# New step orders for the loops of an attention kernel on one core

## The chip, the cores and the metric

One of the eight cores of a Trainium2 chip runs the kernel. The metric is the device time of one execution in microseconds (us). A median of several executions is given, and one further execution was recorded by the hardware profiler; that one has its own span, from the first to the last instruction.

## The reference

Thirty-two sequences of different lengths (64 to 511 rows out of 512, 512 columns each) go through a projection to queries, keys and values, and through attention with eight heads of 64. Rows past a sequence's length are zero in the output.

```python
for b in range(batch):                        # 32
    x_b = x[b, :lengths[b]]
    q, k, v = split(x_b @ w_qkv, 3)           # each 8 heads of 64
    scores = q @ k.T / sqrt(64)               # for each head
    attn = exp(scores - max) / sum(exp(scores - max))
    output[b, :lengths[b]] = concat(attn @ v) # the rest of output[b] is 0
```

## The kernel before

**Tiling and stages.** The lengths are sorted on the chip, and the batches are worked on as sixteen pairs, longest first. There is one loop for each width: 512, 448, 384, 352 and so on down to 96 (LOOPS, L236). A loop runs as many times as there are pairs that need its width; for this draw 512, 448, 384, 320, 288, 256, 192, 128 and 96 run once, 224 and 160 twice, and 352 three times. A loop's body has two positions, one for each batch of its pair. A position (L1028) does the attention of its own batch and, between those steps, the projections of the batch that comes next. All inputs of TensorE are 16-bit (f16); its sums lie in eight PSUM banks of 512 columns, numbered 0 to 7.

**The steps.** The order of the steps in a position is written out by hand in a list of words (ORDER, L238 to L278), two positions separated by a bar. Every word is a step of TensorE with the copies or divides that follow it, or a step of another engine. The digits after @ are the banks that it writes.

- `S13@45`: group 13 of the scores, into banks 4 and 5 (L1269, L1259). The matmuls have 64 rows, since a head has 64; two heads run side by side in the two halves of the array's rows. ScalarE then takes the exponential of the banks (L1287).
- `Q2@1`, `K2@2`, `V1@6`: one projection each (q, k or values) as **single** matmuls over all 128 rows, four to a bank of 512 columns (qk at L1429, project at L300; val at L1484, values at L311). One copy takes the result to SBUF (L1442, L1489), on VectorE, or with a star (`K0*@7`) on ScalarE.
- `B1a@27 ... B1b:dd`: the same q and k blocks as **pairs** of 64-row matmuls (half_qk at L1360, halves at L1305, matmuls at L1323), one result in each of two banks. The pair comes in two halves, a and b (or three parts, a to c): a starts the sums and b adds the other rows to the same banks. `U0a ... U0b` are two value tiles as such a pair (half_values, L1379), `V0a ... V0b` a tile in halves, `W` the last value tile that two batches share (L1210 if single). The letters after the colon are the copy engines of the two results: d for VectorE, a for ScalarE.
- `A4@5`: value products (exponentials times values, 65 columns a matmul, the 65th giving the sum) as single 128-row matmuls (av at L1504, L1517). `A1a@67 ... A1b` are two heads, or groups of heads, as 64-row pairs (paired at L1599, L1631). `Z` adds the half-filled last tile (rest at L1544, L1557). VectorE then divides by the sums in three operations, R, U and O: reciprocal (L1706), live rows (L1712) and the product (L1715); if the two banks of a pair follow each other, the three operations serve both banks at once (both_normed at L1663, L1671 to L1693).
- `L` live rows, `P` mask and cast to f16 on GpSimd (L371), `D` load of a later x by DMA, `X` DMA transposes of the cast x (L328), `E0` a few columns that a narrower next loop leaves over (columns_left, L1453; its TensorE work only runs when a loop goes on).

**What sets the order of the engines.** The engines run their own instruction streams and wait for each other by semaphores. A planner (plan_waits, L41) goes through the head, the bodies of the loops and their entries in order (follow, L64), keeps for each bank and buffer who wrote it and who reads it, and plans a wait wherever an operation isn't already known to follow (L134 to L152). To hold in every loop alike, operations are named by rank, counted from the end of their position (by_rank, near L1865): O0 is the last divide of a position, G0 the last copy. A wait is given as a name and a number of positions back:

```python
wait = ("pos", o["name"], b - o["b"])
```

so a wait that a loop's own repetition needs is also carried out in its first iteration, where it stands for the operation of the same rank in the loop before. used_by (L1536) names the exponential buffers that a value product reads.

Of the kernel before, what the change touches and what calls it, by code (L numbers as in the profile page):

```python
# [18 lines left out]
P = 128  # L19
# [21 lines left out]
def plan_waits(head, bodies, entries, rare):  # L41
# [22 lines left out]
    def follow(chain):  # L64
        clock = defaultdict(lambda: defaultdict(int))
        seen = defaultdict(list)
        write, readers = {}, defaultdict(list)
        ahead = chain[0] == "head"
        came = -1 if ahead else chain[0]
        for at, v in enumerate(chain):  # L70
            if v == "head":
                todo = [("head", 0, k, op) for k, op in enumerate(head)]
                first = -1
            else:
                first = 2 * (chain.index(v) - ahead)
                todo = [(v, j, k, op) for j in range(2) for k, op in enumerate(bodies[v][j])]
                if at:
                    since = 0 if chain[at - 1] == "head" else chain[at - 1] + 1
                    lead = [(w, None, k, op) for w in range(since, v + 1) for k, op in enumerate(entries[w])]
                    todo = lead + todo  # L80
            for w, j, k, op in todo:
                b = -1 if v == "head" else 2 * (at - ahead) + (j or 0)
                mine = clock[op.eng]
                if op.skip and op.eng == "PE":
                    mine = defaultdict(int, mine)
# [64 lines left out]
                    learn(o)  # L150
                by = op.name if op.dma else op.eng
                count = (seen[by][-1]["count"] if seen[by] else 0) + 1  # L152
                after = dict(mine)
                after[by] = count
                o = {"name": op.name, "by": by, "count": count, "clock": after, "b": b}
                o |= {"dma": op.dma, "entry": j is None, "skip": bool(op.skip) and op.eng != "POOL" and not op.passed, "order": len(seen["all"])}
# [5 lines left out]
                    readers[r].append(o)  # L162
                for r in op.writes:
                    write[r] = o
                    readers[r] = []

    follow(["head"])
    for v in range(len(bodies)):
# [8 lines left out]
def kernel(  # L177
# [9 lines left out]
    B, MAXS, D = x.shape  # L187
# [15 lines left out]
    def ring(n, shape, dtype, name, pool=const):  # L203
# [32 lines left out]
    LOOPS = [512, 448, *range(384, 64, -32)]  # L236

    ORDER = {  # L238
        512: "L P D S0@12 U0a@65 S1@34 U0b:dd S2@01 B1a@27 S3@34 B1b:dd S4@56 S5@01 A0@3 A1@2 S6@45 B0a@76 "
        "S7@01 B0b:dd S8@23 U1a@54 S9@01 U1b:ad S10@23 B3a@76 S11@45 A2@0 S12@12 B3b:da S13@45 B2a@03 "  # L240
        "S14@12 S15@67 B2b:da A3@5 A4@2 A5@4 A6@0 X A7@7 | L P D S0@12 U0a@36 S1@45 U0b:ad S2@01 B3a@72 "
        "S3@34 B3b:dd S4@01 U1a@56 S5@34 A0@7 S6@01 U1b:dd S7@23 B0a@74 S8@01 B0b:dd S9@56 S10@23 A1@0 "
        "B2a@71 E0@4 S11@56 B2b:dd S12@23 A2@4 S13@56 A3@7 A4@3 S14@12 B1a@04 S15@67 B1b:ad A5@5 A6@3 X "
        "A7@0",
        448: "L P D S12@67 S13@45 B1a@32 S1@67 B1b:da S5@45 B0a@10 S3@67 B2a@23 S4@45 B0b:da B2b:dd S0@45 V1@6 "
        "S2@01 S6@23 S9@45 V2@7 A0@6 A2@0 Z0 S10@12 B3a@73 S7@45 B3b:da S8@12 A1@0 A3@6 S11@45 Z1 V0*@7 "
        "A4@1 A6@5 Z4 A5@4 X A7@7 Z5 | L P S0@23 S12@01 V1*@6 B2a@52 S1@34 B2b:dd S4@67 S3@01 W0@3 D "
        "S13@45 B1a@67 S6@12 B1b:dd S5@45 B0a@30 S2@12 B0b:dd S7@67 S8@45 V0@2 A0@7 A2@0 Z0 S9@45 S11@12 "
        "B3a@36 A3@7 A4@5 A1@4 Z1 S10@12 B3b:aa A5@0 E0@4 A7@1 A6@2 Z4 Z5 V2*@7 X",
        384: "L P D S0@34 B0a@65 B1a@72 S1@34 B0b:ad B1b:ad S2@01 B2a@43 S3@67 B2b:ad S4@01 A0@5 S5@23 B3a@76 "  # L250
        "S6@01 B3b:da S7@34 U0a@52 S8@01 S9@67 U0b:dd S10@34 A2@0 S11@67 A4@5 V2*@1 X A6@6 | L P D S0@23 "
        "B1a@47 S1@01 B1b:ad S2@23 B3a@56 S3@01 B2a@74 S4@23 B3b:dd S5@01 B2b:da A0@3 S6@12 S7@56 A2@4 "
        "U0a@70 S8@12 E0@3 S9@56 U0b:dd S10@12 B0a@43 S11@56 B0b:aa A4@1 A6@0 V2*@2 X",
        352: "L P D S0@56 V2*@4 S1@01 U0a@27 S2@56 S3@34 U0b:dd S4@01 B1a@65 S5@34 B1b:aa S6@01 A0@2 A2@7 "
        "S7@34 B2a@56 S8@01 B2b:aa S9@34 B3a@27 B0a@10 S10@56 B3b:dd S11@34 B0b:ad A4@6 X A6@5 | L P D "
        "S0@01 B0a@42 S1@67 B0b:da S2@01 B2a@53 S3@67 B3a@42 S4@01 B3b:da S5@67 B2b:da S6@01 A0@4 S7@67 "
        "U0a@25 S8@01 S9@34 U0b:ad B1a@10 S10@67 S11@34 B1b:ad A2@5 A4@7 A6@3 V2*@0 X",
        320: "L P D S2@12 S3@67 U0a@45 S4@01 S1@23 U0b:ad B0a@67 S8@12 B1a@30 S0@45 B0b:da B1b:dd S5@12 B3a@45 "
        "S7@67 B3b:da S9@23 A0a@10 S10@56 B2a@47 S6@23 A0b S11@56 B2b:aa A4@3 X A6@6 Z4 | L P S0@45 S7@12 "
        "W0*@7 D S1@34 B2a@50 S4@12 E0@7 B2b:dd S5@34 B3a@67 S2@12 B3b:aa B0a@43 S3@12 B1a@05 S8@67 "  # L260
        "B0b:da S6@12 B1b:ad A0a@76 S11@34 U0a@25 S10@01 A0b S9@34 U0b:aa A4@0 X A6@3 Z4",
        288: "L P D S0@56 B2a@24 S5@01 B2b:aa S3@67 B0a@01 S1@23 S9@45 B0b:dd S2@67 B1a@32 S6@45 B1b:da S4@67 "
        "B3a@10 S11@45 S8@23 B3b:ad U0a@76 A0a@05 S10@34 S7@12 A0b U0b:aa A6@3 X A4@4 Z4 | L P S5@01 "
        "U0a@27 S0@56 S1@01 U0b:dd S2@56 B3a@43 S6@01 B3b:aa W0a@52 D S10@01 E0@7 W0b:da B1a@34 S3@01 "
        "S4@67 B2a@25 B1b:da S8@01 B2b:da A0a@76 S7@34 S9@12 A0b B0a@05 S11@34 B0b:aa A4@1 X A6@7 Z4",
        256: "L P S0@34 U0a@02 S1@56 U0b:aa B0a@17 S2@34 S3@56 B0b A0a@02 B0c:da B1a@34 A0b B1b A1a@67 B1c:ad "
        "X D A1b | L P S0@01 U0a@25 S1@34 U0b:ad B0a@76 S2@01 E0@4 B0b A0a@23 B0c:da B1a@45 S3@01 A0b B1b "
        "A4@6 A6@7 B1c:aa X D",
        224: "L P B0a@30 S0@12 B0b B1a@45 B0c:da S1@67 B1b S2@01 U0a@23 S3@67 B1c:da U0b:da X D A0a@01 A1a@67 "
        "A0b A1b | L P B0a@45 S0@23 B0b B1a@01 S1@23 B0c:ad B1b S2@67 A0a@23 B1c:da U0a@54 S3@67 A0b "  # L270
        "U0b:aa X D A4@6 A6@7",
        192: "L P S0@01 S1@23 V0*@5 B0a@40 S3@67 B0b A0a@53 S2@12 A0b B1a@67 B0c:aa B1b A1a@21 B1c:ad X D A1b "
        "| L P B0a@50 S1@34 B0b S2@67 B0c:da W0@4 S0@12 B1a@03 S3@67 E0@5 B1b A0a@12 B1c:aa A0b A1a@46 "
        "V0a@57 A1b V0b:aa X D",
        160: "L P S0@01 S1@23 V0@5 Q0*@4 A0@0 K0*@7 A2@1 S2@23 Z0 K2*@6 Q2*@7 X D A4@5 A6@2 Z4 | L P S0@34 "
        "S1@67 K2@0 Q2*@1 A0@3 W0*@4 Q0@6 A2@5 K0*@0 Z0 S2@12 V0*@6 X D A4@4 A6@7 Z4",
        128: "L P S0@12 Q0*@6 K0*@0 V0@7 X D A0@6 A4@5 | L P S0@23 E0@7 Q0*@4 K0*@1 A0@34 V0*@2 X D",
        96: "L P S0@56 K0*@7 Q0*@4 V0@0 X D A0@56 | L P S0@12 Q0*@2 K0*@1 V0*@2 X D A0@34",  # L278
    }

    NARROW = (512, 448, 384, 320, 288, 256, 192, 128)
# [746 lines left out]
    def position(N, j, at, ring):  # L1028
# [11 lines left out]
        across = max(1, BANK // wide)  # L1040
# [188 lines left out]
        todo = [(i, kt) for i in range(NH // 2) for kt in range(n - quarters)]  # L1229
        lone = [(i, n - 1) for i in range(0, NH // 2, 2)] if quarters else []  # L1230
        todo = todo + lone
# [304 lines left out]
        def used_by(blocks, late=False):  # L1536
            if packed:
                mine = [todo.index(block) for block in blocks]
                mine = {min(k, len(todo) - 1) // across for b in mine for k in (b, b + 1)}
                return [f"et{j}.{k}" for k in sorted(mine)]  # L1540
            es = sorted({where[b + (0,)][0] for b in blocks})
            return [f"et{e}" for e in es] + [f"et{j}b"] * late
# [359 lines left out]
    def op_of(v, j, k):  # L1902
        return head[k] if v == "head" else (entries[v] if j is None else bodies[v][j])[k]
# [57 lines left out]
    for (v, j, k), todo in waits.items():  # L1961
        op = op_of(v, j, k)
# [81 lines left out]
    with tc.tile_critical():  # L2044
# [38 lines left out]
        for v, N in enumerate(LOOPS):  # L2083
# [17 lines left out]
            body, after = f"loop_{N}", f"after_{N}"  # L2101
            nc.br_lt(pair, ends[v], on_true=body, on_false=after)
            with nc.body(body):
# [6 lines left out]
                for j in range(2):  # L2110
                    for e in EN:
                        mine = [(k, op) for k, op in enumerate(bodies[v][j]) if op.eng == e]
# [54 lines left out]
```

## Time and profile before

| | us |
|---|---|
| median of 3 runs (lowest, highest) | 327.81 (327.38, 327.87) |
| span of the profiled execution | 328.5 |
| TensorE busy | 311.6 (95%) |
| ScalarE busy | 262.6 (80%) |
| VectorE busy | 197.7 (60%) |
| GpSimd busy | 101.9 (31%) |

The profile names the engines PE (TensorE matmuls), PEld (TensorE weight loads), DVE (VectorE), ACT (ScalarE), POOL (GpSimd) and SP (SyncE, which issues the DMAs). A line of the timeline gives the start, the duration, the engine, the line of the kernel, the operation, what it writes and reads, the size and the count; a bracket is the idle time ahead of it and what ended it. TensorE's matmuls are pipelined and their ends are modelled, so its durations overlap with the starts of the next ones. The span was 0.7 us longer than the median of the runs.

### The profile page before, as it was taken

What the parts mean: (1) busy time and instruction counts of PE and PEld (TensorE: products, weight loads), DVE (VectorE), ACT (ScalarE), POOL (GpSimd) and SP (SyncE); (2) the same over time, 40 slices, a digit from 0 to 9 for tenths busy, and PEclk for the clock granted to TensorE, in tenths of its full rate; (3) what the DMA queues carried; (4) which work ended last, traced back from release to release, by engine and by line L of the source; (5) the groups of instructions that cost most, each with busy time, mean ns of one, the idle gap of its engine ahead of it and who ended that gap; (6) DMA issues with size and microseconds to landing.
All of it is one profiled execution on the core that took longest, in us unless ns stands there. A gap on an engine that the chain in (4) does not pass through costs nothing.

```text
span 328.5 us, 13310 instructions
## 1 busy us (share of the span) xinstructions
PE 311.6 (95%) x5092; PEld 202.3 (62%) x5092; DVE 197.7 (60%) x635; ACT 262.6 (80%) x413; POOL 101.9 (31%) x148
## 2 busy tenths in 40 slices
PE   6899999999999999999999999999998999999980
PEld 4444645555655556556656657667777886777860
DVE  6777567566666646456455465545575565776853
ACT  4379999897878988988978989899867779687761
POOL 6448040324030330330231243043222224435320
PEclk9999999999999999999999999999999999999997
DMA  6984749395858999696676766857459857966651
GB/s 217 382 278 80 251 140 327 76 354 153 304 52 298 224 269 258 197 268 224 233 214 224 255 194 205 211 174 242 156 131 227 183 176 164 223 206 177 193 180 66
DMA packets 69449, 68.85 MB, mean 210 GB/s; under 512 B 40720, under 2 KB 40720, under 8 KB 69392
## 3 DMA queue, kind: packets, MB, share of 16 engines
q1 hardware_dynamic: 69344, 68.12, 71.4%
q8 instruction: 33, 0.54, 0.7%
q14 instruction: 24, 0.20, 0.2%
q10 hardware_dynamic: 48, 0.00, 0.0%
HBM read 25.17 MB, written 33.55 MB: 179 GB/s over the span
## 4 chain that ended last, share of the span: by engine, by line
PE 84%; DVE 5%; DMA 3%; issue 2%; ACT 2%; SPq 1%; POOL 1%; DVEq 0%; POOLq 0%; ACTq 0%
PE banks L1323 41%; PE banks L1269 13%; PE banks L1517 12%; PE banks L300 6%; PE banks L311 6%; PE banks L1631 2%; DMA xT<-x 2%; DMA x_nat<-in_x_dram 2%; PE banks L1210 1%; PE banks L1557 1%; DVE out_nat L1715 1%; DVE rcp L1712 1%; DVE out_nat L1693 1%; SPq L328 1%; ACT et L1287 1%
## 5 line engine op out<-in xcount | busy, mean ns | idle before, releaser
L1287 ACT ACTIVATE et<-banks 128x704 f16<-128x704 f32 (+8 forms) x256 | 198.8, 825 | 27.8 <-PE banks L1269 24.7
L371 POOL TENSOR_TENSOR x<-x_nat,mask 128x512 f16<-128x512 f32 x83 | 84.2, 1041 | 184.3 <-DVE mask L1052 174.9
L1323 PE MATMUL banks<-xT,w_r 64*128 64x352 f16 (+9 forms) x1536 | 127.8, 294 | 1.8 <-DMA xT<-x 1.2
L1323 PEld LDWEIGHTS banks<-xT,w_r 64*128 64x128 f16 x1536 | 68.7, 94 | 39.0 <-PE banks L1323 8.5
L1269 PE MATMUL banks<-qz,kT 64*128 64x352 f16 (+11 forms) x624 | 77.5, 294 | 2.6 <-issue 0.7
L1715 DVE TENSOR_TENSOR out_nat<-banks,rcp 128x256 f32<-128x256 f32 (+1 forms) x110 | 53.0, 482 | 3.8
L1367 DVE CAST qz<-banks 128x448 f16<-128x448 f32 (+6 forms) x47 | 26.4, 561 | 45.2 <-PE banks L1323 44.8
L1517 PEld LDWEIGHTS banks<-v_aug,et 128*128 128x128 f16 x1240 | 41.7, 97 | 13.5 <-issue 6.8
L1517 PE MATMUL banks<-v_aug,et 128*128 128x65 f16 x1240 | 47.1, 194 | 0.0
L1323 PE MATMUL banks<-w_r,xT 64*128 64x512 f16 (+1 forms) x368 | 46.6, 372 | 0.3 <-ACT v_aug L1489 0.3
L1269 PEld LDWEIGHTS banks<-qz,kT 64*128 64x128 f16 x624 | 28.1, 93 | 25.9 <-issue 7.1
L1706 DVE RECIPROCAL rcp<-banks 128x4 f32<-128x4 f32 (+1 forms) x112 | 20.3, 181 | 20.7 <-PE banks L1517 7.3
L311 PE MATMUL banks<-w_r,xT 128*128 128x512 f16 x104 | 26.9, 381 | 0.5 <-DVE xT L782 0.5
L1386 DVE CAST v_aug<-banks 128x512 f16<-128x512 f32 x25 | 16.6, 690 | 17.9 <-PE banks L1323 17.9
L1323 PEld LDWEIGHTS banks<-w_r,xT 64*128 64x128 f16 x368 | 17.2, 94 | 14.1 <-PE banks L1323 1.0
L1367 ACT CAST kT<-banks 128x352 f16<-128x352 f32 (+6 forms) x47 | 22.5, 479 | 1.5 <-PE banks L1323 1.5
L300 PE MATMUL banks<-xT,w_r 128*128 128x160 f16 (+3 forms) x256 | 23.0, 243 | 0.5 <-DVE v_aug L1489 0.5
L1367 DVE CAST kT<-banks 128x352 f16<-128x352 f32 (+5 forms) x33 | 17.9, 552 | 7.7 <-PE banks L1323 7.6
L300 PEld LDWEIGHTS banks<-xT,w_r 128*128 128x128 f16 x256 | 16.6, 98 | 5.2 <-DMA xT<-x 0.6
L1367 ACT CAST qz<-banks 128x352 f16<-128x352 f32 (+6 forms) x33 | 15.3, 465 | 3.7 <-PE banks L1323 3.6
L1489 ACT CAST v_aug<-banks 128x512 f16<-128x512 f32 x15 | 8.8, 589 | 9.5 <-PE banks L311 9.5
L1631 PE MATMUL banks<-v_aug,et 64*128 64x65 f16 x624 | 14.2, 190 | 0.6 <-issue 0.6
(116 smaller groups left out, 193.3 us busy)
## 6 DMA issues: line engine op xcount, KB each, us to landing
x_nat<-in_x_dram SPq DMA_DIRECT2D x12, 768.0 KB, 6.4
out_dram<-out_nat SPq DMA_DIRECT2D x12, 768.0 KB, 4.0
x_nat<-in_x_dram SPq DMA_DIRECT2D x14, 512.0 KB, 4.5
out_dram<-zeros SPq DMA_DIRECT2D x12, 512.0 KB, 3.6
out_dram<-out_nat SPq DMA_DIRECT2D x12, 512.0 KB, 4.7
out_dram<-out_nat SPq DMA_DIRECT2D x4, 1024.0 KB, 7.0
x_nat<-in_x_dram SPq DMA_DIRECT2D x3, 1024.0 KB, 5.3
out_dram<-zeros SPq DMA_DIRECT2D x4, 768.0 KB, 4.7
```

The source lines that it names most:

```text
L300: last = nc.tensor.matmul(dst[:, 0:N], w_r[:, c, w0 : w0 + P], xT[:, c, 0:N], start=(c == 0), stop=(c == NC - 1),)
L311: last = nc.tensor.matmul(pv, xT[:, c, t * P : (t + 1) * P], w_r[:, c, 2 * D : 3 * D], start=(c == 0), stop=(c == NC - 1),)
L371: return engine.tensor_tensor(out=x16, in0=x32, in1=live.broadcast_to([P, D]), op=ALU.mult)
L1269: last = nc.tensor.matmul(psc[par][:, x * wide : x * wide + N], kT[r, i, c0 : c0 + P], qz[r, i, 0:N], start=True, stop=True,)
L1287: return nc.scalar.activation(out=et[:, :, x0:x1, 0:N], in_=got.rearrange("p j (x q) -> p j x q", q=wide)[:, :, x0:x1, 0:N], func=AF.Exp, ...
L1323: last = nc.tensor.matmul(to, lhs(rows, c), rhs(rows, c), start=(c == 0 and opens), stop=(c == NC - 1 and not opens),)
L1367: return lambda copy, bank: copy(out=buf[:, ms, 0:M], in_=bank[:, 0 : gm * M].rearrange("p (m q) -> p m q", q=M),)
L1386: return lambda copy, bank: copy(out=v_bufs[o][:, t, :, 0:HD], in_=bank.rearrange("p (h d) -> p h d", d=HD))
L1517: last = nc.tensor.matmul(pav[:, g, qt, :], e_bufs[e][:, c0 + qt * P : c0 + (qt + 1) * P], v_aug[:, kt, h, :], start=(kt == 0 and not (hal ...
L1631: last = nc.tensor.matmul(pavs[own][:, g, qt, :], e_bufs[e][rows, c0 + qt * P : c0 + (qt + 1) * P], (v_bufs[0] if ending else v_aug)[rows, ...
L1706: return nc.vector.reciprocal(out=rcp, in_=pav[:, :, :, HD])
L1715: return nc.vector.tensor_tensor(out=o_t[:, 0:n, h0 * HD : (h0 + heads) * HD].rearrange("p t (g d) -> p g t d", d=HD), in0=pav[:, :, :, 0:HD],
```

## The change

All twelve order lists are new, 224's only in its banks and a few places. In the loops from 512 to 160 columns most projections become single 128-row matmuls where they were 64-row pairs, and a part of the value products becomes 64-row pairs where they were single; the scores come in another order and in other banks; D, P, X and the copies' engines move. Of the planner, two details are changed: an operation that only runs if a loop ends or goes on (skip below 0) no longer passes on what it learnt by its own waits, and such an operation on TensorE no longer clears the list of a bank's readers. In used_by, the index that follows the last block of a position wraps around to the first.

```diff
-                after = dict(mine)
+                after = dict(clock[op.eng] if op.skip < 0 else mine)
...
                     write[r] = o
-                    readers[r] = []
+                    if op.skip >= 0 or op.eng != "PE":
+                        readers[r] = []
...
-        512: "L P D S0@12 U0a@65 S1@34 U0b:dd S2@01 B1a@27 S3@34 B1b:dd S4@56 S5@01 A0@3 A1@2 S6@45 B0a@76 "
...
+        512: "L S13@01 S15@23 S6@45 V1@6 K3@7 S1@01 S4@23 K1*@6 Q0@7 S3@01 S0@45 K0*@2 Q1@3 S7@01 S2@67 S10@45 "
...
-        "S13@45 B1a@67 S6@12 B1b:dd S5@45 B0a@30 S2@12 B0b:dd S7@67 S8@45 V0@2 A0@7 A2@0 Z0 S9@45 S11@12 "
-        "B3a@36 A3@7 A4@5 A1@4 Z1 S10@12 B3b:aa A5@0 E0@4 A7@1 A6@2 Z4 Z5 V2*@7 X",
-        384: "L P D S0@34 B0a@65 B1a@72 S1@34 B0b:ad B1b:ad S2@01 B2a@43 S3@67 B2b:ad S4@01 A0@5 S5@23 B3a@76 "
...
+        "V1@2 W0@3 S12@45 B0a@01 S9@67 S8@23 S7@45 B0b:dd A0@6 A2@7 D Z0 A1a@23 S11@01 S10@45 A1b V0@6 A4@7 "
+        "E0@0 K3@1 A6@2 Z4 X A5@0 A7@1 Z5",
+        384: "L S3@34 B3a@56 V0a@27 S1@34 B3b:da V0b:dd S10@01 S4@34 V1@6 S0@12 B2a@05 S5@34 B0a@67 S2@12 B2b:dd "
+        "S6@34 B0b:da S7@12 Q1@0 S11@45 A0a@67 S8@23 P S9@01 D A0b V2*@4 A4@5 K1*@0 A6@7 X | L Q0*@6 S0@01 "
+        "S2@45 S11@23 Q2@7 V1@6 S1@01 B3a@45 S7@23 E0@7 S9@67 B3b:dd P V0@0 S10@23 S8@67 S6@45 V2*@1 A0@2 "
+        "K0*@0 D S5@67 A1a@45 S4@23 S3@01 A1b K1*@6 K2*@7 A2@3 Q1*@0 X",
...
-        "S0@01 B0a@42 S1@67 B0b:da S2@01 B2a@53 S3@67 B3a@42 S4@01 B3b:da S5@67 B2b:da S6@01 A0@4 S7@67 "
-        "U0a@25 S8@01 S9@34 U0b:ad B1a@10 S10@67 S11@34 B1b:ad A2@5 A4@7 A6@3 V2*@0 X",
-        320: "L P D S2@12 S3@67 U0a@45 S4@01 S1@23 U0b:ad B0a@67 S8@12 B1a@30 S0@45 B0b:da B1b:dd S5@12 B3a@45 "
...
+        "S1@67 A1b K1*@0 A2@1 A0@6 V2*@0 Q2@3 X D",
+        320: "L S0@45 S4@12 S11@67 Q2@0 V0*@3 Q3@5 P S7@01 V1a@67 S1@23 B0a@45 S5@01 V1b:ad D S2@23 B0b:dd S3@01 "
...
+        "S9@67 A2@0 D A0@5 S8@12 S10@34 Z0 V1*@6 A4@7 K2*@1 E0@4 A6@3 X Z4",
+        288: "L S10@45 S1@01 P V1@2 S2@45 S6@67 K0*@1 Q1*@0 Q3@3 S3@45 S7@67 S11@12 V0@0 S9@45 S8@67 K3*@3 K1@2 "
...
-        192: "L P S0@01 S1@23 V0*@5 B0a@40 S3@67 B0b A0a@53 S2@12 A0b B1a@67 B0c:aa B1b A1a@21 B1c:ad X D A1b "
...
+        192: "L S2@12 S3@34 V0@0 Q2*@6 P K0@7 A1a@23 S1@01 S0@45 A1b D K2@6 Q0*@7 A2@0 X A0@1 Z0 | L S3@45 S2@23 "
+        "Q2*@6 W0*@7 P S1@45 S0@01 K2*@2 A4@6 E0@7 K0*@3 D A6@7 A2@5 Z4 V0*@1 A0@4 Q0*@3 X Z0",
+        160: "L S2@12 P Q0*@0 S1@67 K0*@3 K2@2 A6@0 A4@1 Z4 S0@45 V0*@7 Q2*@6 D X A0@2 A2@4 Z0 | L P S0@01 S1@56 "
+        "Q0@3 K0@7 V0*@2 Q2@1 W0@4 S2@23 K2@0 A0a@67 A1a@45 D X A0b A1b",
+        128: "L P V0@0 S0@23 Q0*@1 K0*@4 X D A0@0 A4@1 | L P S0@23 E0@4 Q0*@5 K0*@0 A0@23 V0*@1 D X",
...
-                mine = {min(k, len(todo) - 1) // across for b in mine for k in (b, b + 1)}
+                mine = {(k % len(todo)) // across for b in mine for k in (b, b + 1)}
```

## What I predict

> **What bounds the kernel now.** I began with the page: the span, the busy times, the chain of work that ended last.
>
> ```profile
> span 328.5 us, 13310 instructions
> PE 311.6 (95%) x5092; PEld 202.3 (62%) x5092; DVE 197.7 (60%) x635; ACT 262.6 (80%) x413; POOL 101.9 (31%) x148
> PE 84%; DVE 5%; DMA 3%; issue 2%; ACT 2%; SPq 1%; POOL 1%; DVEq 0%; POOLq 0%; ACTq 0%
> ```
>
> TensorE is busy for 95% of the span and holds 84% of the chain. Then the windows view, cut at the first scores step of each loop; shown are the row of the 352 loop (three pairs of batches: length, then PE, PEld, DVE, ACT, POOL, then clock, DMA share, GB/s) and the sum.
>
> ```profile
> 117.44:189.78 72.34, 72.34 (x1081) 43.28 (x1081) 38.59 (x113) 64.06 (x108) 18.43 (x19) 1.00 0.80 233
> ...
> sum 299.32, PE 292.69 PEld 192.15 DVE 180.85 ACT 251.28 POOL 91.04; mean PE 26.61 PEld 17.47 DVE 16.44 ACT 22.84 POOL 8.28
> ```
>
> The loops take 299.3 us, 292.7 of them with TensorE busy, at full clock. So the question is what the new order does to TensorE: to its streaming, to the gaps between its steps, and to its waits. ScalarE is next, at 251 of 299. The timeline of TensorE (start, length, work, count) gives the first two.
>
> ```profile
> 103.59 1.02 PE L311 MATMUL banks<-w_r,xT 128*128 128x512 f16 x4
> 104.45 0.35 PE L1517 MATMUL banks<-v_aug,et 128*128 128x65 f16 x6
> ...
> 116.48 1.03 PE L311 MATMUL banks<-w_r,xT 128*128 128x512 f16 x4
> 117.44 0.32 PE L1269 MATMUL banks<-qz,kT 64*128 64x352 f16 x2
> 117.70 1.04 PE L311 MATMUL banks<-w_r,xT 128*128 128x512 f16 x4
> ...
> 119.99 1.03 PE L1323 MATMUL banks<-w_r,xT 64*128 64x512 f16 x8
> 120.85 0.31 PE L1269 MATMUL banks<-qz,kT 64*128 64x352 f16 x2
> 121.00 0.76 PE L1323 MATMUL banks<-xT,w_r 64*128 64x352 f16 x8
> 121.60 0.31 PE L1269 MATMUL banks<-qz,kT 64*128 64x352 f16 x2
> 121.83 0.77 PE L1323 MATMUL banks<-xT,w_r 64*128 64x352 f16 x8
> ```
>
> Starts are to be read, not lengths: a listed length holds a modelled end of about 0.17 us that the next step overlaps (two scores are listed at 0.31, the next step starts 0.15 later). Three readings. First, four single 128-row matmuls of 512 columns take 104.45 − 103.59 = 0.86 us; eight 64-row halves of 512 also take 120.85 − 119.99 = 0.86. Both do the same work: a pair of halves runs at once, so **single or paired, a projection streams for the same time**. Second, a **change of row mode costs about 0.1 us**: after two scores (64-row) a single 128-row step starts 0.26 later (117.44 to 117.70), a 64-row one 0.15 later (120.85 to 121.00); and a single step ahead of scores takes 0.96 (116.48 to 117.44), not 0.86. Third, scores laid between the two halves of one pair (121.60, second half at 121.83) take 0.23, not 0.15: the second half adds to the banks of the first and here waits 0.08 for it.
>
> **The change part by part.** The order lists of the twelve loops are replaced; matmuls do the same multiplications. Counted from the lists by step and number of 64- or 128-row matmuls, each loop as often as it runs (512 to 256, 192, 128 and 96 once, 352 three times, 224 and 160 twice): 64-row halves of q and k 1536 to 592, of values 352 to 256; single projections 348 to 864; single value products 1264 to 768, their paired halves 624 to 1640. By the first reading, **streaming: 0**. Bounds: none of the two forms is quicker in any row, so nothing is left here but the rounding of 0.86, 0.01 on 516/4 groups, ±1.3.
>
> *Mode changes.* I went through the lists and counted where a 64-row step (scores, pair part, rest halves) stands next to a 128-row one (single projection, single value product). Before to after, by loop: 512 15–15, 448 22–21, 384 12–13, 352 30–36, 320 7–15, 288 4–20, 256 2–6, 224 3–3, 192 5–11, 160 16–20, 128 3–5, 96 4–4. Together 123 to 169: 46 more, at 0.105 (the mean of 0.26 − 0.155 and 0.96 − 0.86) **+4.8 us**. It lies on TensorE itself, so nothing covers it, unless the step would have waited anyway: bounds 2.4 (half of them fall into waits) and 5.5 (0.12 each).
>
> *Second halves.* From 0.23 − 0.15 a second half starts no sooner than 0.23 after the first ends. Where less work lies between, the missing part is lost: 51 places before, 2.8 us by that rule; 14 after, 0.5. Fewer pairs, and longer work between halves: **−2.2 us** (bounds −3 and −1).
>
> *Entries of loops.* Waits are planned by an operation's rank, counted from the end of a position (O0 is its last divide, G0 its last copy), and a wait needed in a loop's steady state is also made in its first iteration, where it falls on the operation of that rank in the loop before, needed or not. The rows of the entries before:
>
> ```profile
> 60.04 0.93 PE L1323 MATMUL banks<-xT,w_r 64*128 64x448 f16 x8 [0.21 <-DVE out_nat L1715]
> 190.53 1.04 PE L1323 MATMUL banks<-w_r,xT 64*128 64x512 f16 x8 [0.25 <-ACT v_aug L1489]
> 212.32 0.29 PE L1269 MATMUL banks<-qz,kT 64*128 64x288 f16 x2 [0.21 <-DVE out_nat L1715]
> 212.60 0.56 DVE L1715 TENSOR_TENSOR out_nat<-banks,rcp 128x384 f32<-128x384 f32 x1
> 213.31 0.30 PE L1269 MATMUL banks<-qz,kT 64*128 64x288 f16 x2 [0.20 <-DVE out_nat L1715]
> 287.88 0.38 PE L1269 MATMUL banks<-qz,kT 64*128 64x160 f16 x6 [0.23 <-issue]
> 288.62 0.38 PE L1269 MATMUL banks<-qz,kT 64*128 64x160 f16 x6 [0.36 <-DVEq L2042]
> 310.10 0.40 PE L1269 MATMUL banks<-qz,kT 64*128 64x128 f16 x8 [0.25 <-ACT v_aug L1489]
> 317.39 0.35 PE L1269 MATMUL banks<-qz,kT 64*128 64x96 f16 x8 [0.38 <-DVE out_nat L1693]
> ```
>
> The scores at 213.31 write banks that nothing in the loop before held any more; they start just when the last divide, begun at 212.60, has ended at 213.16. That is the rank rule at work. Eight brackets sum to 2.09; each hides the 0.17 of a modelled end, 1.4 more: 3.5 us lost at entries before. For the new lists I named, for each early step, the operation of that rank in the position before, and took its time from these rows:
>
> ```profile
> 91.38 0.18 DVE L1706 RECIPROCAL rcp<-banks 128x4 f32<-128x4 f32 x1 [0.62 <-PE banks L1557]
> ...
> 92.13 0.17 DVE L1706 RECIPROCAL rcp<-banks 128x4 f32<-128x4 f32 x1
> 116.14 0.20 DVE L1706 RECIPROCAL rcp<-banks 128x6 f32<-128x6 f32 x1 [1.00 <-PE banks L1517]
> ...
> 117.05 0.18 DVE L1706 RECIPROCAL rcp<-banks 128x6 f32<-128x6 f32 x1
> 286.34 0.21 DVE L1671 RECIPROCAL rcp<-banks 128x8 f32<-128x8 f32 x1 [1.99 <-PE banks L1631]
> ...
> 287.39 0.17 DVE L1706 RECIPROCAL rcp<-banks 128x4 f32<-128x4 f32 x1
> 290.56 0.43 ACT L1442 CAST qz<-banks 128x320 f16<-128x320 f32 x1 [0.43 <-PE banks L300]
> L1367 DVE CAST kT<-banks 128x352 f16<-128x352 f32 x11 | 5.4, 518 | 3.0 <-PE banks L1323 3.0
> ```
>
> A divide group takes 0.75 us for one tile of 4 heads (91.38 to 92.13), 0.91 for 6 heads (116.14 to 117.05), 1.05 for two banks at once (286.34 to 287.39). Then: 384 begins with S3@34, bank 3 being that of A2@3, whose divide is the last of a 384 position; in the first iteration that is the last of the 448 loop's second position, which ends Z4, A5, A7, Z5: four groups, 3.0, and 0.2 to get going, against 1.05 of TensorE work after Z4: 2.2. 320 begins with scores that wait for the last copy before them, Q2@3 of 352, on VectorE: 0.2 and 0.52 of the last row, 0.8. 288's fifth step S6@67 waits for the last divide of 320: two groups of 0.91 and 0.2 to get going, less 1.3 of the steps ahead of it (V1's 0.86 and three scores), 0.7. 160's S2@12 waits for the copy Q0*@3 on ScalarE, 0.43 and start, 0.5. 128's second steps S0@23 wait for a two-bank divide, two groups of 1.05 after the last value product less V0's 0.86, 1.2. Together 5.4 in place of 3.5: **+1.9 us** (bounds −3.5, all gone, and +4, a second divide late at each). The first scores of 384 hold up all behind them, ScalarE's exponentials included.
>
> *First step of all.* It is S13 in place of S0, and S13 reads block 3 of the keys, which VectorE copies as the second of two:
>
> ```profile
> 21.98 1.29 DVE L822 CAST kT<-banks 128x512 f16<-128x512 f32 x2 [0.35 <-PE banks L300]
> 22.68 0.39 PE L1269 MATMUL banks<-qz,kT 64*128 64x512 f16 x2 [0.31 <-ACT xT L782]
> ```
>
> The copies end at 23.27; scores at 23.4 instead of 22.68: **+0.7 us** (bounds 0 and +1).
>
> *Waits inside positions.* By the same readings 2.0 us before; after, new ones (the first scores of 128's second position 0.6 for the copy K0*, 160's second round 0.3 for a divide, 0.2 each in 512 and 448) come to about as much: **0** (bounds −2 and +2). ScalarE makes 116 copies in place of 138, VectorE 142 in place of 119 and 72 divide operations fewer, since pairs divide two banks at once; neither sets the end in steady state, as both had slack in each window. D, the loads, and P, the cast ahead of the transposes X, move too, past more steps; one wait for a transposed tile is in the trace:
>
> ```profile
> 254.48 0.56 PE L1323 MATMUL banks<-xT,w_r 64*128 64x224 f16 x8 [1.24 <-DMA xT<-x]
> ```
>
> The order of 224 is nearly unchanged, so I let it stand: **0** (bounds −1.4 and +3, a like wait in two more loops). The planner's mended clock and readers and the wrapped buffer index can only add waits that are met early: **0** (0 to +1).
>
> **Sum:** 4.8 − 2.2 + 1.9 + 0.7 = +5.2; 328.5 + 5.2 = 333.7 in a profiled execution. The median of runs, 327.8, lies 0.7 under the profiled span: **333.0 us**.
>
> **The rivals.** *Faster: waits vanish.* The new lists give each copied bank more time before its next use, so that neither a copy nor a divide is ever awaited at entries (−3.5, and −0.7 at two smaller ones, 256 and 192) nor inside (−2.0): 4.8 − 2.2 − 6.2 + 0.7 = −2.9, 324.9 us. It decides once over 4 of these 6.2 us go (3.3 to make good, and 0.65). For it speaks that most waits in the trace are for copies and divides; against it that S3@34 stands first in 384 right behind four divide groups. *Mode changes half hidden*: 2.4 in place of 4.8, 330.6 us; against it, windows with no gap at all, as that of 352, where 6 of the 46 lie. *No change*: half of the waits gone and half of the mode changes hidden, 4.8 − 2.4 − 2.2 − 3.1 + 0.7 + 1.9 of late divides in 384 = −0.3, 327.5. *Transposes late*: D and P later in 320 to 160, two more waits like that at 254.48, 1.4 each: 335.8 us.
>
> A single projection could also pay for its weights, as each of its loads fills the whole array:
>
> ```profile
> L311 PEld LDWEIGHTS banks<-w_r,xT 128*128 128x128 f16 x104 | 8.2, 97 | 10.0 <-issue 1.6 <-DVE xT L782 1.2 <-ACT et L1287 0.4
> ```
>
> 516 more of them at 97 ns in line would be +50 us, 383 us. Four in 0.86 are 215 ns each, the streaming of 512 columns alone (the halves' time as well), so the load is hidden: under 1 in 100. [...]
>
> **How the numbers follow.** Forecast 0.56, with its own range 331 to 335.3 (mode changes ±1, entries and inside waits ±1.5 together); mode changes half hidden 0.12; transposes late 0.08; weights in line under 0.01; no change 0.08; faster 0.15. A measurement of this kernel tells ±0.2%, 0.65 us, from nothing. So faster 0.15, same 0.08, slower 0.77. Range 327.5 to 335.8: left out are the faster case (0.15) and half of the late transposes.
>
> **What would show it.** Each right step has a place: scores of the 384 loop starting some 2 us after the last matmul of 448; the first scores at about 23.4; 0.26 rather than 0.15 from scores to single projections in 288 and 320, and these two loops longer by 1.7 and 0.8 from that alone; 128's S0 over 1 us late; fewer second halves at 0.23. I am wrong if TensorE's gaps at mode changes are gone or if its waits at entries sum to under 2 us.

## The result, and the profile after

The changed kernel takes **342.09 us** (median of 4 runs, 341.06 to 342.93), the kernel before 327.84 (327.38 to 327.90): a ratio of **1.0433, 95% interval 1.0407 to 1.0459**, 14.2 us slower. The forecast of 333.0 had the direction; the size was 5.2 forecast and 14.2 measured, and 342 lies outside the range of 327.5 to 335.8.

The page of the changed kernel: span, busy times, chain. (Its lines behind the order lists have numbers two lower than before: L1267 for L1269, L298 for L300, L1713 for L1715.)

```profile
span 340.7 us, 13257 instructions
PE 315.6 (93%) x5080; PEld 201.2 (59%) x5080; DVE 204.0 (60%) x586; ACT 254.1 (75%) x391; POOL 101.8 (30%) x148
PE 77%; DVE 14%; issue 4%; DMA 1%; ACT 1%; DVEq 0%; SPq 0%; PEld 0%; POOL 0%; PEldq 0%; POOLq 0%; ACTq 0%
```

TensorE is busy 4 us longer, and the span grows by 12. VectorE's share of the chain goes from 5% to 14%: TensorE now waits for it. The windows view of the changed kernel, cut again at the first scores of each loop (384 and 352 shown):

```profile
96.21:123.91 27.70, 27.03 (x397) 16.05 (x398) 14.57 (x35) 21.86 (x33) 6.28 (x7) 0.94 0.64 205
123.91:198.15 74.24, 72.48 (x1131) 42.90 (x1129) 45.55 (x110) 60.03 (x97) 18.37 (x19) 1.00 0.74 222
```

384 grows from 25.1 to 27.7 and has a granted clock of 0.94; 352, with 72.48 of 74.24 busy, has gaps that it did not have (72.34 of 72.34).

One thing about the base. The profiled execution of before was itself an unlucky one: with the same lists (first experiment) the next profile has a span of 326.1; the 1.4 us wait at 254.48 isn't in it, and its first scores begin 0.7 earlier. I compare with that one. From the timelines, going step by step through the lists (start-to-start time less streaming), the loops divide so, in us. (A turn is the passage from one position to the next; half clock is a granted clock of 0.50.)

```
                                 lists of before   changed    differ   forecast
loops, all                            297.7         311.6     +13.9
 streaming                            268.4         268.4       0         0
 changes of row mode (0.107 each)     123 = 13.2    169 = 18.1 +4.9      +4.8
 second halves that wait                2.2           0.4      -1.8      -2.2
 waits at entries of loops              4.5           8.3      +3.8      +1.9
 other waits (turns of positions)       9.0          12.6      +3.6       0
 TensorE at half clock                  0             1.7      +1.7       -
 stalls inside a step, no releaser      0.5           2.1      +1.6       -
first scores begin at                  22.0          22.8      +0.8      +0.7
```

The first three forecast lines came out. The other 9 us are what the experiments are about.

### The profile page after: what moved, and what is told of

Its sections match the earlier page's. It is cut to its first block, busy times and chain, and to the rows that moved or that the text cites. A ratio compares the mean times of both kernels' runs of the same rounds, so it can differ in the third digit from the quotient of the medians.

```text
span 340.7 us, 13257 instructions
## 1 busy us (share of the span) xinstructions
PE 315.6 (93%) x5080; PEld 201.2 (59%) x5080; DVE 204.0 (60%) x586; ACT 254.1 (75%) x391; POOL 101.8 (30%) x148
## 4 chain that ended last, share of the span: by engine, by line
PE 77%; DVE 14%; issue 4%; DMA 1%; ACT 1%; DVEq 0%; SPq 0%; PEld 0%; POOL 0%; PEldq 0%; POOLq 0%; ACTq 0%
PE banks L298 23%; PE banks L1321 19%; PE banks L1267 14%; PE banks L309 7%; PE banks L1629 7%; PE banks L1515 4%; DVE out_nat L1713 3%; DVE out_nat L1691 3%; DVE rcp L1710 2%; DVE rcp L1678 2%; PE banks L1208 1%; DMA x_nat<-in_x_dram 1%; DVE rcp L1704 1%; DVE rcp L1669 1%; PE banks L1555 1%
## 5 line engine op out<-in xcount | busy, mean ns | idle before, releaser
L298 PE MATMUL banks<-xT,w_r 128*128 128x352 f16 (+10 forms) x728 | 101.0, 283 | 0.5 <-issue 0.5
L1267 PE MATMUL banks<-qz,kT 64*128 64x352 f16 (+11 forms) x624 | 70.5, 296 | 10.5 <-DVE out_nat L1713 4.1
L298 PEld LDWEIGHTS banks<-xT,w_r 128*128 128x128 f16 x728 | 56.6, 98 | 33.3 <-issue 4.5
L1267 PEld LDWEIGHTS banks<-qz,kT 64*128 64x128 f16 x624 | 25.5, 94 | 40.3 <-issue 14.6
L1321 PE MATMUL banks<-xT,w_r 64*128 64x224 f16 (+6 forms) x592 | 46.7, 286 | 0.6 <-issue 0.3
L1629 PEld LDWEIGHTS banks<-v_aug,et 64*128 64x128 f16 x1640 | 30.5, 94 | 6.0 <-issue 0.9
L1629 PE MATMUL banks<-v_aug,et 64*128 64x65 f16 x1640 | 33.1, 190 | 0.4 <-issue 0.4
L1321 PEld LDWEIGHTS banks<-xT,w_r 64*128 64x128 f16 x592 | 27.6, 95 | 9.4 <-issue 1.1
L1713 DVE TENSOR_TENSOR out_nat<-banks,rcp 128x256 f32<-128x256 f32 (+1 forms) x62 | 30.0, 484 | 2.1
L1515 PE MATMUL banks<-v_aug,et 128*128 128x65 f16 x744 | 29.5, 194 | 0.9 <-issue 0.9
L1440 DVE CAST qz<-banks 128x352 f16<-128x352 f32 (+6 forms) x41 | 21.9, 535 | 14.0 <-PE banks L298 13.0
L1691 DVE TENSOR_TENSOR out_nat<-banks,rcp 128x512 f32<-128x512 f32 (+1 forms) x36 | 27.5, 765 | 1.2
```

The costliest lines, as they stand in the source:

```text
L298: last = nc.tensor.matmul(dst[:, 0:N], w_r[:, c, w0 : w0 + P], xT[:, c, 0:N], start=(c == 0), stop=(c == NC - 1),)
L1267: last = nc.tensor.matmul(psc[par][:, x * wide : x * wide + N], kT[r, i, c0 : c0 + P], qz[r, i, 0:N], start=True, stop=True,)
L1321: last = nc.tensor.matmul(to, lhs(rows, c), rhs(rows, c), start=(c == 0 and opens), stop=(c == NC - 1 and not opens),)
L1440: return copy_on(act)(out=buf[:, ms, 0:M], in_=bank[:, 0 : gm * M].rearrange("p (m q) -> p m q", q=M),)
L1515: last = nc.tensor.matmul(pav[:, g, qt, :], e_bufs[e][:, c0 + qt * P : c0 + (qt + 1) * P], v_aug[:, kt, h, :], start=(kt == 0 and not (hal ...
L1629: last = nc.tensor.matmul(pavs[own][:, g, qt, :], e_bufs[e][rows, c0 + qt * P : c0 + (qt + 1) * P], (v_bufs[0] if ending else v_aug)[rows, ...
```

## The experiments

**1. The planner alone** (lists of before, new planner and index).

> The kernel before with the changed planner and the changed buffer index, all order lists as before. My theory: the planner's part costs nothing, so 0 (within 0.65 us of the kernel before). The rival, that the mended planner adds waits that are met late: +1 to +4 us. It also shows whether the 1.4 us wait for a transposed tile (the row at 254.48 of before) and the 0.8 us stall of TensorE in the 192 loop without a releaser (at 284.9 to 285.7) belong to every execution: if so, its profile has both at the same steps; if they were mishaps of that one execution, its span is about 2 us shorter than 328.5.

Measured: 328.64 us against 328.17, ratio 1.0015 (0.9991 to 1.0039): **no difference**. The stall in the 192 loop recurs, with 0.5 us in place of 0.8; the wait for the transposed tile doesn't; each loop but 224 and 192 is as long as before within 0.1 us, and the span is 326.1.

```profile
span 326.1 us, 13310 instructions
```

**2. Changes of row mode alone.** On the kernel before, in 352, all pairs of projections to singles, for example:

```diff
-"... S4@01 B1a@65 S5@34 B1b:aa S6@01 ..."
+"... S4@01 Q1*@6 S5@34 K1*@5 S6@01 ..."
```

> The kernel before, old planner, with one part of the change alone: in the 352 loop each 64-row pair of projections becomes two single 128-row ones at the places of its two halves, same banks, same copy engines, scores and value products untouched. That makes 96 more changes between 64-row and 128-row steps (32 in each of three iterations) and takes away 18 second halves that waited 0.05 each (0.16 in each position). Theory of mode changes at 0.105: +10.1 - 1.0 = +9.1 us, nearly all in the 352 loop (72.3 to about 81.4). Rival, mode changes hidden and the loss of the new lists being waits alone: -1 to 0. Rival, weight loads in line with their streams, 240 single matmuls more in each iteration at 97 ns: +70 us. Half-hidden mode changes: +4.

Measured: 337.36 us, ratio 1.0278 (1.0247 to 1.0310), **+9.2 us** where 9.1 were expected. Window of its 352 loop, and the start of it in TensorE's timeline:

```profile
116.68:198.52 81.84, 81.84 (x841) 40.94 (x841) 39.17 (x113) 65.70 (x108) 18.41 (x19) 1.00 0.70 214
```

```profile
117.91 0.32 PE L1269 MATMUL banks<-qz,kT 64*128 64x352 f16 x2
118.16 1.04 PE L311 MATMUL banks<-w_r,xT 128*128 128x512 f16 x4
119.13 0.47 PE L1269 MATMUL banks<-qz,kT 64*128 64x352 f16 x4
```

81.84 in place of 72.34, busy without a gap in the windows view: the cost of a change is invisible as idle time. It is in the starts: 0.25 from scores to projection, 0.97 from projection to scores. The single matmuls added, 80 in each of three iterations (the 240 of the expectation is their sum; at 97 ns in line they would be 23 us), cost nothing beside it, so no weight load stands in line.

**3. The entry of 384.** On the changed kernel:

```diff
-448: "... A1b V0@6 A4@7 E0@0 K3@1 A6@2 Z4 X A5@0 A7@1 Z5"
+448: "... A1b V0@6 A2a@45 E0@0 K3@7 A2b X A3a@01 A3b"
-384: "... K2*@7 A2@3 Q1*@0 X"
+384: "... K2*@7 A2@2 Q1*@0 X"
```

> The changed kernel with two edits that shorten what its 384 loop waits for at its entry: the last four value products of the 448 loop go as two 64-row pairs whose divides serve two banks at once, and the last value product of a 384 position takes bank 2 instead of 3, so that the first scores no longer share a bank with the last divide. In the changed kernel's trace these scores wait 2.2 us (2.18 idle at 96.21), and TensorE's granted clock then is 0.50 from about 97 to 100. Theory, rank-planned wait and a clock that falls after the idle time: wait under 0.8, no half clock behind it, so -1.5 to -1.9 from the wait and about -1.7 from the clock, together -3 to -3.6 against the changed kernel (339 where that has 342). Rival, that the half clock has nothing to do with the idle time: -1.5 to -1.9 and a stretch at 0.50 still there. Rival, that the wait only moves on to the next steps: 0 to -0.5.

Measured: 340.93 us, 1.2 less than the changed kernel; the sum expected was missed. The place itself did as expected. Changed kernel first: the scores at the entry of 384, then two windows of 3.41 us, the second of them the whole stretch at half clock.

```profile
96.21 0.34 PE L1267 MATMUL banks<-qz,kT 64*128 64x384 f16 x2 [2.18 <-DVE out_nat L1713]
```

```profile
93.43:96.84 3.41, 1.23 (x28) 0.90 (x26) 2.69 (x11) 0.26 (x1) 0.00 (x0) 1.00 0.51 115
96.84:100.25 3.41, 3.41 (x30) 2.44 (x26) 0.33 (x1) 1.70 (x3) 0.00 (x0) 0.50 0.42 151
```

After 2.18 us without work TensorE runs at a granted 0.50 for 3.41 us: 1.7 lost.

What the 14 traces of this case show is this. In each, the changes of the granted clock lie whole multiples of 3.413 us apart (in the changed kernel at 4.68, 96.84, 100.25 and 335.77: 27, 1 and 69 times); I count each trace in steps of that length from its own first change (4.68 here, 6.82 in before). Over the 14 traces, at full clock, TensorE fell to 0.50 behind each of the 21 steps in which it had 1.95 us or more without a matmul, and behind none of the 1301 steps with 1.78 or less. (14 of the 21 are at the end of the kernel, one is in a head, six are in the loops. In the changed kernel they have 2.18 and 2.42 us and in before 2.98; no other full step of these two has over 1.23.) Here the 2.18 us of idle time lie whole in the step from 93.43 to 96.84.

The experiment: the entry, the window behind it, and then the entry of the 224 loop and the window behind that.

```profile
95.50 0.34 PE L1269 MATMUL banks<-qz,kT 64*128 64x384 f16 x2 [0.26 <-DVE out_nat L1693]
...
255.64 0.42 DVE L1715 TENSOR_TENSOR out_nat<-banks,rcp 128x256 f32<-128x256 f32 x1
...
256.62 0.56 PE L1323 MATMUL banks<-xT,w_r 64*128 64x224 f16 x8 [2.14 <-DVE out_nat L1715]
```

```profile
94.70:98.70 4.00, 3.74 (x65) 2.39 (x66) 2.67 (x7) 2.15 (x4) 0.00 (x0) 1.00 0.64 70
256.60:260.60 4.00, 3.98 (x49) 3.88 (x51) 0.37 (x3) 0.96 (x2) 2.04 (x2) 0.57 1.03 179
```

The wait fell to 0.45 (0.26 idle), and the clock stayed at 1.00: rank wait and half clock confirmed at 384. But 2.3 us were now lost at the entry of 224, where the changed kernel loses 0.3, with a half clock behind them (a granted 0.57 over the window from 256.60 to 260.60). VectorE's divide, which the row names, had ended at 256.06, and TensorE moved only 0.56 later: that releaser is not the whole cause. Experiment 6 shows a cause that fits. The profiled execution is one of the two longest of the six runs (343.4 us each; the other four took 340.4 to 341.0), so this loss isn't shown for the four. They too lie at most 0.7 under the shortest run of the changed kernel, 341.06: the gain of 3 us is missing in all six, and for the four the record doesn't show where it went.

**4. New lists in parts.** The new lists for 512 to 384, for 352 to 256, and for 224 to 96, the others as before.

> The changed kernel with the new lists for 512, 448 and 384 alone, the lists of before from 352 on. By the two traces these three loops took 36.6, 33.1 and 25.1 us before and 38.2, 35.2 and 27.7 after, though mode changes there are hardly more (49 in both) : +6.3 us if the loss lies in these loops themselves (entry wait, half clock, stalls), so about 334. If their loss depended on what follows, or the shortfall were one execution's mishap: +2 to +3.

> The changed kernel with the new lists for 352, 320, 288 and 256 alone, all other lists as before. By the traces of the kernel before (planner changed) and after, these loops took 72.3, 21.5, 21.1 and 14.1 us, and then 74.2, 21.5, 21.6 and 14.8: +3.1 us, though 41 of the 46 added mode changes lie here, 4.4 us, since the waits for second halves and at entries of 320 and 288 went down. If the parts add up: +3 to +3.5. If mode changes cost nothing there: -1.

> The changed kernel with the new lists for 224, 192, 160, 128 and 96 alone. By the same traces: 27.3, 12.6, 22.2, 7.3 and 4.6 before, 28.2, 13.0, 23.9, 8.7 and 4.7 after, +4.4 us, of which 1.2 are mode changes (11) and the rest waits at the turns from one position to the next (for the divides, the copies, and P's cast). If the parts add up: +4 to +4.8. If the small loops' loss came from what the large ones leave behind (loads and transposes that are late): +1.5.

Measured: **+8.3 us** (ratio 1.0226, 1.0157 to 1.0296), **+3.8** (1.0115, 1.0089 to 1.0141) and **+3.8** (1.0123, 1.0091 to 1.0155). Middle and small lie within 0.7 of what the traces gave. The large ones lose 2 more than by the traces, but their four runs lie in two groups: 334.1 and 334.7, which is +6.2 as the traces had it, and 338.3 and 338.8. The profile is of the last; in it TensorE stands idle for 2.97 us at the entry of the 160 loop, whose list is that of before, and then does 6.1 us of work at half clock, about 3 us lost:

```profile
293.88 0.98 PE L1269 MATMUL banks<-qz,kT 64*128 64x160 f16 x12 [2.97 <-issue]
```

```profile
293.16:299.98 6.82, 6.10 (x54) 4.59 (x55) 0.87 (x3) 2.99 (x5) 2.94 (x4) 0.50 0.69 171
```

The sum, 15.9, is above the whole, 14.2; with the two lower runs of the large lists it is 13.8. The entry of 384 has the same idle time in this profile as in the changed kernel, without a fall of the clock. Counted back from 293.16, a border between two steps of the clock falls at 95.18, inside the idle time, so that 1.34 us of it lie in one step and 0.85 in the next:

```profile
96.03 0.34 PE L1269 MATMUL banks<-qz,kT 64*128 64x384 f16 x2 [2.19 <-DVE out_nat L1715]
```

```profile
91.77:95.18 3.41, 2.07 (x55) 1.66 (x53) 3.17 (x13) 0.00 (x0) 0.00 (x0) 1.00 0.29 66
95.18:98.59 3.41, 2.56 (x38) 1.96 (x40) 1.18 (x5) 1.74 (x3) 0.00 (x0) 1.00 0.24 55
```

**5. The cast, P, early again.** On the changed kernel, in all positions:

```diff
-352: "L K1*@1 S0@45 S8@23 S10@67 Q3@0 Q2@1 K3@4 P D S6@23 ..."
+352: "L P K1*@1 S0@45 S8@23 S10@67 Q3@0 Q2@1 K3@4 D S6@23 ..."
```

> The changed kernel with one edit: the step P (mask, and cast on GpSimd) stands right behind L at the start of each position again, as in the kernel before; all else as changed. In the changed kernel's trace 14 of VectorE's live-row products (lines 1710 and 1678) take 0.27 to 1.04 us in place of 0.17, 7.0 us too much in all (before: 8, 2.9), and nearly all of these lie under a cast of GpSimd of 1.04 us. Theory: VectorE's product waits out the cast, the divide behind it is late, and TensorE waits for the bank or for the copy behind it: 0.95 in the second and third iteration of 352, 0.55 and 0.18 in 384, 0.83 in 192, 0.67 in 160, and 0.4 of the 1.2 at the entry of 320. With P early these go: the long products down to about 3 us, and -2.5 to -3.6 us, about 339 in place of 342. Rival, the long products are long for another reason (what they read, or their place in the queue): still about 14, and 0. Rival, they shorten, but TensorE then waits for the next late thing: products short and 0 to -1.

Measured: 339.23 us, **−2.9** against the changed kernel, as expected; five long products in place of 14, 2.1 us too much in place of 7.0. The changed kernel at the end of an iteration of 352, GpSimd and VectorE, and TensorE's scores that follow:

```profile
143.87 3.04 POOL L369 TENSOR_TENSOR x<-x_nat,mask 128x512 f16<-128x512 f32 x3 [13.00 <-DVE mask L1050]
...
145.11 0.83 DVE L1678 TENSOR_TENSOR rcp<-rcp,v_aug 128x12 f32<-128x12 f32 x1
...
148.65 0.51 DVE L1440 CAST qz<-banks 128x352 f16<-128x352 f32 x1
...
149.22 0.47 PE L1267 MATMUL banks<-qz,kT 64*128 64x352 f16 x4 [0.30 <-DVE qz L1440]
```

and the same with P early:

```profile
144.11 0.17 DVE L1680 TENSOR_TENSOR rcp<-rcp,v_aug 128x12 f32<-128x12 f32 x1
...
147.09 0.52 DVE L1442 CAST qz<-banks 128x352 f16<-128x352 f32 x1
```

```profile
122.90:195.66 72.76, 72.14 (x1130) 43.23 (x1127) 43.70 (x111) 60.01 (x97) 18.41 (x19) 1.00 0.83 226
```

The product of 12 numbers a partition takes 0.83 while a cast of GpSimd runs and 0.17 without; counted from this product's start the last copy begins 0.56 later (3.54 in place of 2.98), and the next scores wait. Without it 352 takes 72.76 in place of 74.24. This is the largest part of "other waits". What holds the product back is not shown; the rows show the 0.83, under casts of 1.04 each. Each of the 14 long products of the changed kernel ends 0.01 to 0.03 us after an operation of GpSimd has ended, 12 of them after a cast and two after a copy, and none that began under a cast was short.

**6. The same work at other places in the code.** On the changed kernel, 40 matmuls more among those of the head whose bank nobody reads (`warm`):

```diff
+op("warm1c", "PE", lambda: [nc.tensor.matmul(banks[3][:, 0:16], ones16, ones16[:, 0:16], start=True, stop=True) for _ in range(40)][-1], (), ("bk3",))
```

> The changed kernel with 40 small matmuls more among the warming ones of the head, where TensorE is idle anyway (6.7 to 7.8 us), into a bank that nobody reads: no work changes behind it, only the place of each instruction in TensorE's code, by 80 instructions. In the traces so far TensorE stalls in the middle of a step, without a releaser, at the same two steps of the new lists in each run: in A0 of 512's second position (1.07, 1.29, 0.77 us) and A2a of 448's first (0.60, 0.75, 0.88), and each such stall ends 1.4 to 1.7 us after a 16 KB load of TensorE's code ended. Theory, TensorE waits for its code where a load's border falls among value products, which use up instructions quickest: the two stalls are no longer at these steps; the time changes by -1.8 to +1, by where the borders fall now. Rival, the stall is for data or for the transposes issued just before it (X stands beside both steps): both stay where they are, 0.

Measured: 343.67 us, ratio 1.0465 (1.0413 to 1.0517) to the kernel before, 1.6 over the changed kernel where −1.8 to +1 was expected; the two ratios' intervals overlap. First the end of 512's second position in the changed kernel. ("issue" in a bracket: the engine waited for nothing that the profile shows.)

```profile
58.28 1.04 PE L1515 MATMUL banks<-v_aug,et 128*128 128x65 f16 x29
...
60.22 0.74 PE L1515 MATMUL banks<-v_aug,et 128*128 128x65 f16 x19 [0.91 <-issue]
```

Then the DMA view of the changed kernel from 57.60 to 60.30, with the one packet of code in it (queue q8; packets, MB, share). The page of the changed kernel has 33 packets on this queue, 0.54 MB or 16 KB each. That it is TensorE's is my estimate from counts, as TensorE has by far the most instructions: in the 512 loop 584 matmuls and 585 weight loads, VectorE 54 operations, ScalarE 39.

```profile
q8 instruction: 1, 0.02, 2.0%
```

And the shifted kernel:

```profile
58.15 1.62 PE L1517 MATMUL banks<-v_aug,et 128*128 128x65 f16 x48
...
75.99 0.34 PE L299 MATMUL banks<-xT,w_r 128*128 128x384 f16 x1
78.96 1.30 PE L299 MATMUL banks<-xT,w_r 128*128 128x384 f16 x7 [2.63 <-issue]
```

The 48 value products now run through without a break, and the stall in 448's first position is gone too. In their place stand 2.8 us in the middle of K1* in 448's second position (after its first matmul), 0.8 in 320 and 1.5 in 224; the steps' data and transposes are the same. So these stalls belong to **places in the code**, as expected, and a shift moves them; 5.0 us in place of 2.1 in these profiles. In the traces each ends 1.3 to 1.8 us (once 2.0) after a 16 KB packet of this queue has ended (the one in the view above lasted from 57.75 to 58.63, work began again at 60.22), whatever the step. Other idle times named "issue", 0.3 to 0.5 us at three steps of the last loops, follow no packet; the shift left them where they were, and they are not counted here. Most of the 33 packets are followed by no such stall, but a few are, by one of up to 2.8 us. The 2.3 us at 224 in experiment 3 fit this too (1.76 after its packet; with three more, this profile has 5.3 us of such stalls where the changed kernel has 2.1), and so does the idle time at 160 in experiment 4 (1.5 after).

**7. Both mends together.** Experiments 3 and 5 in one kernel.

> The changed kernel with both mends together: P early, and the shorter entry wait of 384 (two 64-row pairs at the end of 448, bank 2 for the last value product of 384). If the terms add up: -2.9 as measured for P early, -1.9 for the wait and -1.7 for the half clock behind it, so 342.1 - 6.5 = 335.6, and what is left over the kernel before, some 7.5 us, is mode changes (4.9), the other entries and turns (3 to 4), code loads (1 to 2), less the second halves (1.8). If the gain of the shorter entry is always given back by a code load, as in its first run: 338 to 339.

Measured: 342.65 us (340.88 to 344.49), where 335.6, or 338 to 339 with a code stall, was expected: both failed. Its loops do show the mends: 448 and 384 together 60.1 us in place of 62.9, 352 72.8 in place of 74.2, all loops 308.8 in place of 311.6. But the entry of 224 has the code stall of experiment 3 again, with the half clock behind (a granted 0.61 from 257.70 to 261.70; the code up to there is as long), and its head took 4.1 us longer in this profile, where two pieces of VectorE's work lasted 3.4 and 3.2 us under a clearing by GpSimd of 3.2. The same clearing lies over them in the changed kernel, where they last 0.7 and 0.4; why they stood here stays open.

```profile
257.71 0.56 PE L1323 MATMUL banks<-xT,w_r 64*128 64x224 f16 x4 [2.66 <-issue]
```

**8. A version meant to beat both.** Lists of before with steps shifted and banks exchanged where TensorE waits at entries.

> A version meant to beat both: the lists of before (pairs as they are), with steps shifted by a few places and banks exchanged where the traces show TensorE waiting, and P early: 117 changes between 64-row and 128-row steps in place of 123 (-0.6 us), the entry waits of the loops 448, 320, 288, 160 and 128 (about 0.4, 0.4, 1.0, 0.9 and 0.4 us in the profile with the lists of before) down to about a third of their 3.1 (-2.0), second halves as before or 0.4 worse; the planner is the changed one. Theory of the terms: -2 us, 326 where before has 328. Rival, that the chance of where code loads fall (so far 0.5 to 5.0 us in a profile, 0.5 to 0.8 with the lists of before) outweighs it: -1 to +2. Rival, that waits only move on: 0.

> The first tuned version lost where the step E0 had been moved ahead of steps that use its bank, or ahead of a divide: TensorE waited 1.8, 1.6, 1.3, 0.7 and 0.5 us there for E0's clearing on VectorE (row L1479). Here E0 stands at least a step of its bank later, all else by the same rules: 119 mode changes in place of 123 (-0.4), entry waits of 448, 320, 288 and 160 down by some 1.7 in all, waits inside about as before. Theory: -1.5 to -2.5 us against the kernel before, none of the waits for L1479 above 0.5. Rival, code loads fall worse: 0 to +2. Rival, other late operations take their place: 0 and more.

> The lists of tuned_e0 from 352 on, those of before for 512, 448 and 384. Theory: the entry waits of 320, 288 and 160 are where most of the gain lies (1.3 of 1.7), so -1 to -2 us. Rival as in tuned_e0.

Measured: 334.94 us (ratio 1.0222, 1.0168 to 1.0276), 329.94 (1.0070, 1.0042 to 1.0098) and 329.99 (1.0062, 1.0039 to 1.0084): **none beats the kernel before**, and the last two are 0.6 to 0.7% longer. The first lost where E0 had come near steps of its bank:

```profile
48.40 0.39 PE L1269 MATMUL banks<-qz,kT 64*128 64x512 f16 x2 [1.74 <-DVE kT L1479]
```

With E0 later these waits are down to 0.25 at most, but the loops take 298.7 us against 297.7 with the lists of before: second halves 2.6 in place of 2.2, and the waits removed at entries came back within positions of 352, 192 and 128. Waits moved on, as one rival said.

## Why the prediction was right in direction and wrong in size

- **Streaming, 0**: right; 268.4 us in both.
- **Mode changes, +4.8**: right, 46 at 0.107 = 4.9, and experiment 2 shows the price alone (9.2 us for 96 of them, less the second halves). The rivals "half hidden" and "weights in line" are out.
- **Second halves, −2.2**: −1.8.
- **First scores, +0.7**: +0.8; the row names the copy of the keys, as the step said.

```profile
22.81 0.82 PE L1267 MATMUL banks<-qz,kT 64*128 64x512 f16 x6 [1.04 <-DVE kT L820]
```

- **Entries, +1.9**: the mechanism was right (384 loses 2.36 where 2.2 was worked out, 288 0.7 for 0.7, 160 0.5 for 0.5, 128 1.1 for 1.2), but the term was half of what came. 320 lost 1.2 for 0.8, since a cast delayed the divides ahead of its copy (0.7 with P early); and I had counted only the five entries with a large wait: 256, 224, 192 and 96 have 0.6, 0.3, 0.6 and 0.7.

```profile
198.15 0.58 PE L1267 MATMUL banks<-qz,kT 64*128 64x320 f16 x6 [1.16 <-DVE qz L1440]
...
329.72 0.34 PE L1267 MATMUL banks<-qz,kT 64*128 64x96 f16 x8 [0.68 <-ACT v_aug L1487]
```

- **Waits inside positions, 0, bounds −2 and +2**: the step that failed outright; +3.6. Its working took VectorE's durations from rows of before, where P stands first in every position and its casts rarely meet a divide (8 long products, 2.9 us). That D and P move past more steps was costed by the transposes alone; what was not asked is which engine's work the cast would now lie over. That neither ScalarE nor VectorE sets the end, "as both had slack in each window", is a statement on means: VectorE is busy for 60% of the span and holds 14% of the chain, since single operations of it come late. Experiment 5 takes 2.9 us away, 0.5 of them at the entry of 320, so some 2.4 of the 3.6; the other 1.2 stay open. The 2.0 us put down for these waits before were brackets alone, which hide 0.17 each and leave out short gaps; step by step they are 9.0.
- **Nothing was put down for the clock and the code**: 1.7 and 1.6 us. A wait of 2.2 us was forecast at 384 and priced at 2.2; its price was 3.9 in that execution, with the half clock. That part belongs to the execution and not to the order: in experiment 4 the same wait, 2.19 us across a border of the steps of 3.413 us, was followed by a clock of 1.00. And though the change shifts every instruction, the sum has no term for stalls at places of the code.
- **The planner, 0**: right (experiment 1). Late transposes, the rival on the far side, are not what happened: in the changed kernel's trace no wait that the profile lists for TensorE in the loops is for a transposed tile.

Together 1.9 + 3.6 + 1.7 + 1.6 make 8.8 of the 9.0 us that the forecast lacked. The 1.7 and 1.6 belong to one execution, so the closeness of this sum is in part luck. What stays open is which code packets are followed by a stall; the runs show that a few are, not the rule.

## What to carry to other kernels

When TensorE is busy nearly all the time, count the changes between its tiling shapes in the new order: each cost 0.1 us here, and the views above count it as busy time. When a step on another engine moves, ask what it will run beside, not only what waits for it: a cast on GpSimd turned 0.17 us on VectorE into up to 1.0. And price a wait of some 2 us on TensorE above its length: half clock followed the 2.18 us at 384 here and took 1.7 more, though it did not follow the 2.19 in experiment 4. And expect a rewrite of a program as long as this one to move stalls at places of the code by a few us either way: the profiles here have 0.5 to 5.3 us of them.

## What the runs showed of the hardware that I had not expected

- VectorE's small product of live rows took 0.17 us alone and 0.27 to 1.04 when it ran into a cast or copy of GpSimd, and then ended 0.01 to 0.03 us after that operation (14 of them, 7.0 us too much, in the changed kernel; 5, 2.1 us, with P early).
- TensorE stood idle for 0.4 to 2.8 us at places in its code, in the middle of steps or at entries, each time until 1.3 to 2.0 us after a 16 KB packet of queue q8 had ended, and at other steps when 80 instructions were added ahead.
- In the 14 traces TensorE's granted clock changed only at whole multiples of 3.413 us from its first change, and half clock followed the steps with 1.95 us or more of idle time (21 of 21) and none with 1.78 or less (0 of 1301). So of idle times of 2.1 to 3.0 us in the loops, six brought 0.50 for one step, or in experiment 4 at 160 for two; the other two, 2.19 and 2.63 us, lay across a border (1.34 and 0.85 at 384 in experiment 4, 0.85 and 1.78 in K1* in experiment 6) and brought none.
